# A decoder layer's layer norms read from PSUM on VectorE, and its output projection with two chunks per weight

## The chip, the cores and the metric

The kernel runs on one core of a Trainium2 chip. The metric is the device time of one execution in microseconds. In the text TensorE is PE in the profile, VectorE is DVE, ScalarE is ACT, GpSimd is POOL, and SyncE, which issues the DMAs, is SP.

## What is computed

One layer of a decoder trunk on 1056 tokens (1024 of a prompt, 32 of eight samples), width 1024, in float32:

```
x = LN1(alpha*x + 0.5*SwiGLU_1(x))         # FFN width 2816
m = mixer(x)                               # gMLP branch and gated DeltaNet branch, gated sum
x = LN2(alpha*x + m @ w_out)
y = LN3(alpha*x + 0.5*SwiGLU_2(x))

def layer_norm(x, g, b):
    mu = mean(x); var = mean((x - mu)**2)
    return (x - mu) * rsqrt(var + 1e-5) * g + b
```

## The kernel before

Activations lie with the features on the partitions: eight tiles of 128 features, each 1056 tokens wide. The tokens are cut into three chunks of `C` = 352. Chunk 2 (`LONE`) goes by itself, chunks 0 and 1 (`PAIR`) go together in the FFNs, where a scheme with fewer products combines both. Every product is made of three matmuls of a high and a low part (`mm3`: high by high, low by high, high by low), so every weight and every activation is split: `wh` is the rounded copy made by ScalarE, `wl` the rest, made by GpSimd or DVE. A unit is one weight of 128x1024 for one chunk, 24 matmuls.

The program is written out by one generator for all engines, in the order in which its own clock expects the work. Background generators (`ln_gen` is the one of a layer norm) are stepped between matmuls when that clock passes their due time, so the norm of one chunk is spread between the matmuls of the next. `tt()` gives an addition to GpSimd when its modelled end there, less a slack, is earlier, and to DVE else. At run time each engine goes through its own list in order.

There are nine layer norms: three norms by three chunks. Each works on the accumulator tile of its chunk (named `acc` in the first, `m` in the later norms), eight tiles of 128x352:

- `sum_step` adds the tiles, two at a time (704 wide), into `ss`, while the last products arrive; at the end the two halves of `ss` are added.
- A matmul of `ss` with a matrix of ones gives the column sums `mu` on every partition, in PSUM. ScalarE copies them, scaled by -1/1024, to `mus` in SBUF.
- Four additions of 704 columns subtract the mean (`tt()`, so DVE or GpSimd). ScalarE squares each into `lsq`; the four squares are added up, then the two halves.
- Three matmuls with a column of ones give the sums of squares per token, `vr` (128 tokens on partitions, three columns). DVE computes the inverse root on 128x3 tiles in SBUF (`vx`, `vy`, `vt`): twelve operations, three Newton steps.
- DVE writes three diagonals `dg` (the identity times a column of `vy`), and three matmuls with ones spread them to every partition: `rs`. ScalarE copies `rs` to `rss`.
- Eight scalings by `rss` and the gain: six on DVE, two on GpSimd (a product and then gain and bias). `emit1`, `emit2` and `emit3` then add the bias and split or store the result: `x1h`/`x1l` for the mixer, `x2h`/`x2l` for FFN 2, `y` to HBM.

The norms that matter below: LN1 of chunks 0 and 1 falls into the start of the mixer, where the projections of chunk 2 run and then the small beta and decay projection (`bd`, 16 matmuls) of chunk 0 needs `x1l`. LN2 belongs to the output projection, which goes through the chunks in the order 2, 0, 1 and for each through the eight weights `wo`, 24 units. LN1 and LN3 of chunk 2 fall into the start of the pair's work (the pair starts). LN3 of chunks 0 and 1 is the tail, in which TensorE has nothing else to do.

Of the kernel before, what the change touches and what calls it, by code (L numbers as in the profile page):

```python
# [12 lines left out]
F32 = mybir.dt.float32  # L13
# [8 lines left out]
P = 128  # L22
# [4 lines left out]
NC = 3  # L27
# [12 lines left out]
S0, S1 = 0.2, 0.4  # L40
NPL = 2, 2, 2
# [219 lines left out]
class Kern:  # L261
    def __init__(self, nc, tc, I, O, scratch=None):
# [8 lines left out]
        self.sct, self.scw, self.scn, self.vdone, self.zdone, self.odone, self.omm = {}, {}, {}, 0, 0, 0, 0  # L271
        self.n = 0
# [164 lines left out]
    def sum_step(self, f, c):  # L437

        if f % 2 == 0 or f == 1:
            return  # L440
# [1739 lines left out]
```

## Time and profile before

| | us |
|---|---|
| median of 3 runs | 2880.83 (2880.27 to 2881.67) |
| profiled execution | 2885.94 |
| its span | 2884.2 |
| TensorE busy | 2757.4 (96%) |
| DVE, ScalarE, GpSimd busy | 1746.9, 1110.6, 1449.5 |

The span is the time from the first to the last instruction that the profiler recorded; 1.7 us of the profiled execution lie outside it. Busy is the sum of an engine's instructions, and idle time counts only where the engine that sets the end (here TensorE nearly everywhere) waits for another.

### The profile page before, as it was taken

Reading aid. Unit: us, or ns where it says so; the run is one execution under the profiler, and the core shown is the slowest. Engines: PE = TensorE matmul, PEld = TensorE weight load, DVE = VectorE, ACT = ScalarE, POOL = GpSimd, SP = SyncE. Lnnn points to the kernel's source line nnn. Section 1 sums busy time; section 2 is a strip of 40 time slices with the busy share of each in tenths; the row PEclk is TensorE's granted clock in tenths of the full one; section 3 lists DMA queues with packets and bytes.
Section 4 is the critical chain, followed back from the end, with each engine's and each line's share of the span. In section 5 each row is a group of like instructions: output and inputs, shape, how many; then the busy total and the mean of one; then the engine's idle time right before and its main releaser. Section 6 shows DMA issues by size and latency. Waiting matters only on the chain. (4 is left out here: it accounts for less than half of the span.)

```text
span 2884.2 us, 44396 instructions
## 1 busy us (share of the span) xinstructions
PE 2757.4 (96%) x17467; PEld 2712.6 (94%) x17467; DVE 1746.9 (61%) x2602; ACT 1110.6 (39%) x2215; POOL 1449.5 (50%) x836
## 2 busy tenths in 40 slices
PE   8998999999899998998999999999989989999995
PEld 8998899999899998997999999999989989999995
DVE  4645765554867978997355445036885467554546
ACT  4433433333435655322542433224443334334332
POOL 5556665666526554344124133142466566656663
PEclk9999999999999999999999999999999999999997
DMA  6343122212237988433435287375334422322211
GB/s 228 129 155 97 59 94 74 88 59 74 77 88 161 183 188 155 129 112 133 118 109 165 87 293 268 125 255 188 125 110 139 139 88 65 96 65 88 75 58 40
DMA packets 236863, 358.98 MB, mean 124 GB/s; under 512 B 72144, under 2 KB 169040, under 8 KB 236272
## 3 DMA queue, kind: packets, MB, share of 16 engines
q1 hardware_dynamic: 236656, 356.16, 41.2%
q8 instruction: 137, 2.24, 0.3%
q14 instruction: 70, 0.57, 0.1%
HBM read 279.19 MB, written 76.91 MB: 123 GB/s over the span
## 5 line engine op out<-in xcount | busy, mean ns | idle before, releaser
L166 POOL TENSOR_TENSOR wl<-w,wh 128x1024 fp32r<-128x1024 f32 x220 | 563.8, 2573 | 779.4 <-ACT wh L166 589.4
L386 PE MATMUL ps<-x1h,wh 128*128 128x352 f32 x1536 | 514.7, 335 | 0.0
L388 PE MATMUL ps<-x1h,wl 128*128 128x352 f32 x1536 | 500.6, 326 | 2.2 <-POOL wl L166 2.2
L387 PE MATMUL ps<-x1l,wh 128*128 128x352 f32 x1536 | 499.8, 325 | 0.0
L388 PE MATMUL ps<-h,wl 128*128 128x352 f32 x1056 | 342.3, 324 | 4.6 <-POOL wl L166 4.6
L166 POOL TENSOR_TENSOR s<-w,s 128x512 fp32r<-128x512 f32 x168 | 234.7, 1410 | 218.8 <-ACT s L166 218.8
L386 PE MATMUL ps<-h,wh 128*128 128x352 f32 x1056 | 343.3, 325 | 0.3 <-ACT h L166 0.3
L166 ACT CAST wh<-w 128x1024 fp32r<-128x1024 f32 (+1 forms) x257 | 262.5, 1042 | 90.4 <-PE ps L387 49.8
L386 PEld LDWEIGHTS ps<-x1h,wh 128*128 128x128 f32 x1536 | 292.7, 191 | 4.8 <-issue 1.4
L388 PEld LDWEIGHTS ps<-x1h,wl 128*128 128x128 f32 x1536 | 292.1, 190 | 3.1 <-POOL wl L166 3.1
L387 PEld LDWEIGHTS ps<-x1l,wh 128*128 128x128 f32 x1536 | 292.5, 190 | 0.1
L387 PE MATMUL ps<-h,wh 128*128 128x352 f32 x704 | 228.2, 324 | 0.9 <-DVE h L166 0.9
L166 ACT CAST s<-w 128x512 fp32r<-128x512 f32 x220 | 130.8, 617 | 203.7 <-DVE w L166 101.5
L388 PEld LDWEIGHTS ps<-h,wl 128*128 128x128 f32 x1056 | 198.8, 188 | 5.9 <-POOL wl L166 5.9
L386 PEld LDWEIGHTS ps<-h,wh 128*128 128x128 f32 x1056 | 199.0, 188 | 1.4 <-ACT h L166 0.9
L386 PE MATMUL A<-T,s 128*128 128x352 f32 x528 | 174.5, 331 | 19.2 <-ACT T L166 6.6
L387 PE MATMUL A<-T,s 128*128 128x352 f32 x528 | 172.6, 327 | 1.0 <-DVE T L166 1.0
L388 PE MATMUL A<-T,s 128*128 128x352 f32 x528 | 172.5, 327 | 0.0
L166 DVE TENSOR_TENSOR p<-p,B 128x352 f32<-128x352 f32 x44 | 22.9, 520 | 222.5 <-PE B L388 222.5
L166 DVE TENSOR_TENSOR m<-m,ps 128x352 f32<-128x352 f32 x248 | 120.3, 514 | 54.3 <-PE ps L388 54.0
L387 PEld LDWEIGHTS ps<-h,wh 128*128 128x128 f32 x704 | 132.9, 189 | 1.4 <-DVE h L166 1.4
L166 DVE TENSOR_TENSOR acc<-acc,ps 128x352 f32<-128x352 f32 x224 | 108.0, 514 | 40.6 <-PE ps L388 40.5
(470 smaller groups left out, 7156.6 us busy)
## 6 DMA issues: line engine op xcount, KB each, us to landing
w<-in_wu SPq DMA_DIRECT2D x176, 512.0 KB
w<-in_wd SPq DMA_DIRECT2D x88, 512.0 KB
w<-in_wm SPq DMA_DIRECT2D x64, 512.0 KB
w<-in_wo SPq DMA_DIRECT2D x24, 512.0 KB
acc<-in_xt SPq DMA_DIRECT2D x12, 352.0 KB
scr_x<-acc SPq DMA_DIRECT2D x12, 352.0 KB
scr_z<-z SPq DMA_DIRECT2D x24, 176.0 KB
scr_ga<-tg SPq DMA_DIRECT2D x24, 176.0 KB
```

The lines of the kernel that those rows point to most:

```text
L166: return f(*a, **kw)
L386: nc.tensor.matmul(ps[:, :C], lh, xh, start=(start and i == 0), stop=False, skip_group_check=not start)
L387: nc.tensor.matmul(ps[:, :C], lh, xl, start=False, stop=False, skip_group_check=not start)
L388: nc.tensor.matmul(ps[:, :C], ll, xh, start=False, stop=(i == n - 1), skip_group_check=not start)
```

## The change

The layer norm is rewritten, and the output projection reordered:

- `sum_step` and all sums of squares are on DVE, none on GpSimd. In the very last norm (LN3 of chunk 1) the two halves of `ss` and of the squares are not added: `mu` and `vr` take each half in a matmul of its own.
- The subtraction reads `mu` straight from PSUM, on DVE, with the factor -1/1024 in the same operation. `mus` is gone.
- The inverse root keeps `x` and `t` in unused columns of the PSUM tile `vr`; only `y` is in SBUF. The count of operations stays at twelve, with the operands of a Newton step in another order.
- The diagonals are gone: `rs` comes from a matmul whose stationary operand is a column of `y` spread by its access pattern and whose moving operand is the identity.
- All eight scalings are on DVE and read `rs` from PSUM. `rss` is gone. GpSimd's share of the bias goes to ScalarE.
- The output projection does chunk 2 with the eight weights, and then chunks 0 and 1 together, each weight for both: 16 units loaded and split, not 24. The factor 0.5 moves from the split to the addition of the result (`m<-ps,m`).

Over the whole program: DVE gets 36 subtractions from PSUM where it had 21 and GpSimd 15, 27 sums of squares 704 wide (17 and 10), 72 scalings (54, GpSimd 18), no diagonals (27), and no scaled weight splits (24). ScalarE loses 9 `mus`, 9 `rss` and 24 scaled weight copies for 16 plain ones. GpSimd makes 234 of the weight splits, not 220. SyncE issues eight loads of 512 KB fewer. TensorE has the same 15,312 large matmuls.

```diff
@@ rsqrt
-            nc.vector.tensor_tensor(out=t, in0=y, in1=y, op=ALU.mult)
-            nc.vector.scalar_tensor_tensor(out=t, in0=t, scalar=-0.5, in1=x, op0=ALU.mult, op1=ALU.mult)
+            nc.vector.tensor_tensor(out=t, in0=x, in1=y, op=ALU.mult)
+            nc.vector.scalar_tensor_tensor(out=t, in0=t, scalar=-0.5, in1=y, op0=ALU.mult, op1=ALU.mult)
@@ sum_step
-        self.tt(self.ssum[c], self.acc4(0, c)[:, 0:2] if f == 3 else self.ssum[c], a, ALU.add, S0)
-        if f == 7:
-            self.tt(self.ssum[c][:, 0], self.ssum[c][:, 0], self.ssum[c][:, 1], ALU.add, 0.0)
+        v = self.nc.vector
+        v.tensor_tensor(out=self.ssum[c], in0=self.acc4(0, c)[:, 0:2] if f == 3 else self.ssum[c], in1=a, op=ALU.add)
+        if f == 7 and not self.ending(c):
+            v.tensor_tensor(out=self.ssum[c][:, 0], in0=self.ssum[c][:, 0], in1=self.ssum[c][:, 1], op=ALU.add)
@@ ln_gen
+        halves = 2 if which == 2 and c == ORD[-1] else 1
-        nc.tensor.matmul(mu[:, :C], self.ones, self.ssum[c][:, 0], start=True, stop=True)
+        for i in range(halves):
+            nc.tensor.matmul(mu[:, :C], self.ones, self.ssum[c][:, i], start=(i == 0), stop=(i == halves - 1))
-        mus = self.small("mus")
-        nc.scalar.activation(mus, mu[:, :C], AF.Copy, scale=-1.0 / 1024)
...
+        mub = mu[:, :C].unsqueeze(1).to_broadcast([P, 2, C])
+        for i in range(4):
+            a = self.acc4(i // 2, c)[:, i % 2 * 2:i % 2 * 2 + 2]
+            v.scalar_tensor_tensor(out=a, in0=mub, scalar=-1.0 / 1024, in1=a, op0=ALU.mult, op1=ALU.add)
...
-        x, y, t = self.tiny("vx", 3), self.tiny("vy", 3), self.tiny("vt", 3)
+        y = self.tiny("vy", 3)
+        x, t = vr[:, 8:11], vr[:, 16:19]
-        dg = [self.small("dg", P) for _ in range(3)]
-        for i in range(3):
-            v.tensor_scalar(out=dg[i], in0=self.ident, scalar1=y[:, i:i + 1], scalar2=None, op0=ALU.mult)
-        yield slack[2]
+        yield 1.2 + slack[2]
-            nc.tensor.matmul(rs[:, o:o + n], self.ones, dg[i][:, 128 - n:128], start=True, stop=True)
+            nc.tensor.matmul(rs[:, o:o + n], y[:, i:i + 1].to_broadcast([P, P]), self.ident[:, 128 - n:128], start=True, stop=True)
-        rss = self.small("rss")
-        nc.scalar.copy(rss, rs[:, :C])
...
+            v.scalar_tensor_tensor(out=a, in0=a, scalar=self.prm[:, o:o + 1], in1=rs[:, :C], op0=ALU.mult, op1=ALU.mult)
@@ mix_specs
-        for c in range(NC):
+        for i in range(2):
             for j in range(8):
-                out.append((I["wo"][j].rearrange("p k c -> p (k c)"), 1024, 0.5, ("o", c * 8 + j)))
+                out.append((I["wo"][j].rearrange("p k c -> p (k c)"), 1024, 1.0, ("o", i * 8 + j)))
@@ mixer, output projection
-        for i, c in enumerate(ORD):
+        for i, cs in enumerate(((LONE,), PAIR)):
...
+                for c in cs:
+                    def evac_o(ps, f=f, c=c):
+                        a = self.accv(f, c)
+                        v.scalar_tensor_tensor(out=a, in0=ps[:, 0:C], scalar=0.5, in1=a, op0=ALU.mult, op1=ALU.add)
+                        self.sum_step(f, c)
+                    self.unit_piece(ui, MM, c, evac_o)
```

Three places in DVE's list, before and after. The first is the tail, from the last additions of chunk 1 to the first inverse root; `m_277x` and `m_275x` are the accumulators, `ps` a finished product. Before:

```order
L166 TENSOR_TENSOR m_2780_17932<-m_2780_17932,ps_26819 128x352
L166 TENSOR_TENSOR m_2779_17931<-m_2779_17931,mus_26842 128x2x352
L166 TENSOR_TENSOR m_2780_17932<-m_2780_17932,mus_26842 128x2x352 x2
L166 TENSOR_TENSOR m_2780_17932<-m_2780_17932,ps_26832 128x352
L166 TENSOR_TENSOR ss_4105_26827<-ss_4105_26827,m_2780_17932 128x704
L166 TENSOR_TENSOR m_2780_17932<-m_2780_17932,ps_26847 128x352
L166 TENSOR_TENSOR m_2780_17932<-m_2780_17932,ps_26866 128x352
L166 TENSOR_TENSOR ss_4105_26827<-ss_4105_26827,m_2780_17932 128x704
L166 TENSOR_TENSOR ss_4105_26827<-ss_4105_26827 128x352
L166 TENSOR_TENSOR lsq_26851<-lsq_26851,lsq_26853 128x704
L166 TENSOR_TENSOR lsq_26851<-lsq_26851 128x352
L166 TENSOR_TENSOR m_2779_17931<-m_2779_17931,mus_26890 128x2x352
```

After:

```order
L164 TENSOR_TENSOR m_2759_17890<-m_2759_17890,ps_26729 128x352
L164 TENSOR_TENSOR ss_4034_26691<-ss_4034_26691,m_2759_17890 128x704
L164 TENSOR_TENSOR lsq_26706<-lsq_26706,lsq_26707 128x704
L164 TENSOR_TENSOR lsq_26706<-lsq_26706,lsq_26708 128x704
L164 TENSOR_TENSOR lsq_26706<-lsq_26706,lsq_26707 128x704
L164 TENSOR_TENSOR lsq_26706<-lsq_26706 128x352
L164 SCALAR_TENSOR_TENSOR m_2758_17889<-mu_26749,m_2758_17889 128x2x352 x2
L164 SCALAR_TENSOR_TENSOR m_2759_17890<-mu_26749,m_2759_17890 128x2x352 x2
L164 TENSOR_TENSOR lsq_26752<-lsq_26752,lsq_26753 128x704
L164 TENSOR_TENSOR lsq_26752<-lsq_26752,lsq_26754 128x704
L164 TENSOR_SCALAR vr_26763<-vr_26763 128x3 x2
L164 TENSOR_SCALAR vy_26769<-vr_26763 128x3
```

Before, three subtractions of chunk 0 stood ahead of chunk 1's last two sums, a fourth was on GpSimd, and the squares of chunk 0 were added up partly there. After, all four subtractions are in this list ahead of the rows shown, all sums of squares too, and the 352-wide sum of `ss` is gone.

The second place is the start of the mixer, behind the inverse root of LN1 of chunk 0. `x1l` is the low part of the normalised chunk 0, and `lsq_739x` and `lsq_734x` are sums of squares of chunk 1. Before:

```order
L166 TENSOR_TENSOR acc_1_83<-acc_1_83,mus_7355 128x2x352
L166 TENSOR_TENSOR acc_2_84<-acc_2_84,mus_7355 128x2x352
L166 TENSOR_TENSOR lsq_7391<-lsq_7391,lsq_7392 128x704
L166 SCALAR_TENSOR_TENSOR acc_1_83<-acc_1_83,prm,rss_7441 128x352 x4
L166 SCALAR_TENSOR_TENSOR acc_2_84<-acc_2_84,prm,rss_7441 128x352 x2
L166 TENSOR_TENSOR wl_1133_7463<-w_1112_7341,wh_1132_7462 128x1024
L166 TENSOR_TENSOR lsq_7393<-lsq_7393,lsq_7392 128x704
L166 SCALAR_TENSOR_TENSOR x1l_1137_7497<-acc_1_83,prm,x1h_1136_7481 128x352 x4
L166 SCALAR_TENSOR_TENSOR x1l_1137_7497<-acc_2_84,prm,x1h_1136_7481 128x352
L166 TENSOR_TENSOR lsq_7391<-lsq_7391,lsq_7393 128x704
L166 TENSOR_TENSOR lsq_7391<-lsq_7391 128x352
L166 SCALAR_TENSOR_TENSOR x1l_1137_7497<-acc_2_84,prm,x1h_1136_7481 128x352
```

After:

```order
L164 TENSOR_TENSOR lsq_7345<-lsq_7345,lsq_7346 128x704
L164 TENSOR_TENSOR lsq_7345<-lsq_7345,lsq_7347 128x704
L164 TENSOR_TENSOR lsq_7345<-lsq_7345,lsq_7346 128x704
L164 TENSOR_TENSOR lsq_7345<-lsq_7345 128x352
L164 SCALAR_TENSOR_TENSOR acc_1_83<-acc_1_83,prm,rs_7442 128x352 x4
L164 SCALAR_TENSOR_TENSOR acc_2_84<-acc_2_84,prm,rs_7442 128x352 x4
L164 SCALAR_TENSOR_TENSOR x1l_1122_7472<-acc_1_83,prm,x1h_1121_7466 128x352 x4
L164 TENSOR_SCALAR vr_7476<-vr_7476 128x3 x2
L164 TENSOR_SCALAR vy_7488<-vr_7476 128x3
```

Before, six scalings and six `x1l` stood here among chunk 1's sums, and chunk 1's inverse root came behind the last `x1l`. After, all sums of chunk 1's squares come first, then eight scalings, four `x1l`, and chunk 1's inverse root (from the last row on, twelve operations) ahead of the other four.

The third place is the start of FFN 2, with LN2 of chunks 0 and 1; `u` and `h` are the SiLU of chunk 2. Before, behind the inverse root of chunk 0:

```order
L166 TENSOR_SCALAR dg_19754<-cst,vy_19738 128x128
L166 SCALAR_TENSOR_TENSOR u_19792<-t_19791,ps_19692 128x352
L166 TENSOR_TENSOR u_19792<-u_19792,ps_19723 128x352
L166 SCALAR_TENSOR_TENSOR h_3006_19683<-u_19792,h_3006_19683 128x352
L166 TENSOR_TENSOR m_2779_17931<-m_2779_17931,mus_19775 128x2x352
L166 TENSOR_TENSOR m_2780_17932<-m_2780_17932,mus_19775 128x2x352 x2
L166 SCALAR_TENSOR_TENSOR m_2779_17931<-m_2779_17931,prm,rss_19818 128x352 x4
L166 SCALAR_TENSOR_TENSOR m_2780_17932<-m_2780_17932,prm,rss_19818 128x352 x2
L166 TENSOR_TENSOR lsq_19798<-lsq_19798,lsq_19799 128x704
L166 TENSOR_TENSOR wl_3043_19879<-w_3014_19721,wh_3042_19878 128x1024
```

After, from the `mu` of both chunks on:

```order
L164 TENSOR_TENSOR wl_2951_19564<-w_2936_19439,wh_2950_19563 128x1024
L164 SCALAR_TENSOR_TENSOR m_2758_17889<-mu_19596,m_2758_17889 128x2x352 x2
L164 SCALAR_TENSOR_TENSOR m_2759_17890<-mu_19596,m_2759_17890 128x2x352 x2
L164 SCALAR_TENSOR_TENSOR m_2758_17889<-mu_19625,m_2758_17889 128x2x352 x2
L164 SCALAR_TENSOR_TENSOR m_2759_17890<-mu_19625,m_2759_17890 128x2x352 x2
L164 TENSOR_TENSOR lsq_19608<-lsq_19608,lsq_19609 128x704
L164 SCALAR_TENSOR_TENSOR u_19664<-t_19663,ps_19571 128x352
L164 TENSOR_TENSOR u_19664<-u_19664,ps_19604 128x352
L164 SCALAR_TENSOR_TENSOR h_2947_19558<-u_19664,h_2947_19558 128x352
L164 TENSOR_TENSOR lsq_19608<-lsq_19608,lsq_19610 128x704
L164 TENSOR_TENSOR lsq_19608<-lsq_19608,lsq_19609 128x704
```

Before, the norm of chunk 0 had begun in the output projection, and the one of chunk 1 followed it. After, both begin in FFN 2, with the subtractions of both chunks in one row. At the two pair starts, in the same way, the eight scalings of chunk 2's norm now stand in the list between a SiLU's product with `p` and its product with `A`.

## Rows read from the trace of the kernel before

**Rows 1.** The page, busy time of each engine, share of the span, instructions.

```profile
PE 2757.4 (96%) x17467; PEld 2712.6 (94%) x17467; DVE 1746.9 (61%) x2602; ACT 1110.6 (39%) x2215; POOL 1449.5 (50%) x836
```

**Rows 2.** TensorE's waits in the whole run: us in total, times, longest.

```profile
PE rs L508 <- DVE dg L166: 24.6, 8, 8.2
```

**Rows 3.** Timeline of the tail: start us, us, engine, line, operation; idle time in brackets.

```profile
2842.56 4.01 DVE L166 TENSOR_TENSOR m<-m,mus 128x704 f32<-128x704 f32 x3 [1.05 <-ACT mus L166]
...
2845.58 0.32 PE L388 MATMUL ps<-h,wl 128*128 128x352 f32 x1
...
2845.80 1.47 ACT L166 ACTIVATE lsq<-m 128x704 f32<-128x704 f32 x2 [1.46 <-DVE m L166]
...
2852.33 1.54 PE L457 MATMUL mu<-ss,cst 128*128 128x352 f32 x2 [6.44 <-DVE ss L166]
...
2865.08 1.44 PE L496 MATMUL vr<-cst,lsq 128*128 128x1 f32 x6
...
2873.42 5.14 POOL L166 TENSOR_TENSOR m<-m,rss 128x352 f32<-128x352 f32 x1 [4.62 <-ACT rss L166]
...
2874.40 3.06 DVE L166 SCALAR_TENSOR_TENSOR m<-m,prm,rss 128x352 f32<-128x352 f32 x6
...
2875.08 2.06 ACT L166 ACTIVATE y<-m,prm 128x352 f32<-128x352 f32 x4 [1.09 <-DVE m L166]
...
2881.26 0.41 SPq L2093 DMA_DIRECT2D out_y<-m  x1
```

**Rows 4.** DVE operations by form: ns min/median/max, first and last start us.

```profile
L166 DVE TENSOR_TENSOR m<-m,ps x248: 504/514/524, 1985.8 to 2849.5; 128x352 f32<-128x352 f32 x124
...
L166 DVE SCALAR_TENSOR_TENSOR m<-m,prm,rss x36: 573/580/2724, 2040.9 to 2876.9; 128x352 f32<-128x352 f32 x36
...
L166 DVE TENSOR_TENSOR m<-m,mus x14: 877/886/2398, 2020.5 to 2857.5; 128x704 f32<-128x704 f32 x14
...
L166 DVE SCALAR_TENSOR_TENSOR vt<-vt,vx x30: 160/161/2267, 353.2 to 2869.8; 128x3 f32<-128x3 f32 x27, 128x9 f32<-128x9 f32 x3
...
L166 DVE TENSOR_SCALAR vx<-vr x9: 147/152/161, 349.9 to 2866.6; 128x3 f32<-128x3 f32 x9
```

**Rows 5.** Start of the mixer: TensorE's waits, two windows (busy, count, clock), DVE's timeline.

```profile
PE rs L508 <- DVE dg L166: 5.0, 1, 5.0
...
PE ps L413 <- DVE x1l L166: 4.0, 4, 2.0
...
778.80:785.60 6.80, 3.77 (x14) 3.77 (x15) 6.47 (x15) 2.60 (x5) 2.57 (x2) 0.50 0.00 0
...
792.50:806.10 13.60, 11.60 (x41) 9.15 (x41) 7.27 (x22) 0.55 (x1) 1.44 (x2) 0.50 0.01 1
...
770.57 0.46 DVE L166 TENSOR_TENSOR lsq<-lsq 128x352 f32<-128x352 f32 x1
...
772.14 2.34 DVE L166 TENSOR_SCALAR vt<-vx 128x3 int32<-128x3 int32 x1
...
796.59 0.58 DVE L166 SCALAR_TENSOR_TENSOR x1l<-acc,prm,x1h 128x352 fp32r<-128x352 f32 x1
```

**Rows 6.** Output projection and start of FFN 2: TensorE's waits, one window.

```profile
PE rs L508 <- DVE dg L166: 6.1, 3, 3.6
...
PE ps L388 <- DVE wl L166: 2.6, 3, 1.3
...
PE ps L388 <- POOL wl L166: 2.4, 3, 1.5
...
2123.70:2130.50 6.80, 4.36 (x16) 4.37 (x17) 5.80 (x17) 1.75 (x3) 0.67 (x1) 0.50 0.00 1
```

**Rows 7.** First pair start: TensorE's waits, the window behind them.

```profile
PE A L386 <- ACT p L166: 3.2, 2, 2.3
...
PE rs L508 <- DVE dg L166: 0.6, 1, 0.6
...
359.00:365.80 6.80, 5.91 (x20) 5.91 (x21) 5.91 (x8) 3.89 (x7) 5.32 (x5) 0.50 0.27 100
```

More of the change, by code (lines that the diff above doesn't have):

```diff
@@ L486, in ln_gen @@
-        self.cur = self.pet
-        self.tt(sq[2], sq[2], sq[1], ALU.add, S1)
-        yield (max(ends[2], self.cur),)
-        self.cur = self.pet
-        self.tt(sq[0], sq[0], sq[2], ALU.add, S1)
-        self.tt(sq[0][:, 0], sq[0][:, 0], sq[0][:, 1], ALU.add, 0.0)
+                v.tensor_tensor(out=sq[0], in0=sq[0], in1=sq[(0, 1, 2, 1)[i]], op=ALU.add)
+        if halves == 1:
+            v.tensor_tensor(out=sq[0][:, 0], in0=sq[0][:, 0], in1=sq[0][:, 1], op=ALU.add)
         yield (self.cur + slack[1],)
@@ L495, in ln_gen @@
         for i, o in enumerate((0, 128, C - 128)):
-            nc.tensor.matmul(vr[:, i:i + 1], sq[0][:, 0, o:o + 128], self.ones[:, 0:1], start=True, stop=True)
+            for k in range(halves):
+                nc.tensor.matmul(vr[:, i:i + 1], sq[0][:, k, o:o + 128], self.ones[:, 0:1], start=(k == 0), stop=(k == halves - 1))
         self.pe(1, 0.65)
         yield
-        x, y, t = self.tiny("vx", 3), self.tiny("vy", 3), self.tiny("vt", 3)
+        y = self.tiny("vy", 3)
+        x, t = vr[:, 8:11], vr[:, 16:19]
         v.tensor_scalar(out=x, in0=vr[:, 0:3], scalar1=1.0 / 1024, scalar2=1e-5, op0=ALU.mult, op1=ALU.add)
         self.rsqrt(y, x, t)
-        dg = [self.small("dg", P) for _ in range(3)]
-        for i in range(3):
-            v.tensor_scalar(out=dg[i], in0=self.ident, scalar1=y[:, i:i + 1], scalar2=None, op0=ALU.mult)
-        yield slack[2]
+        yield 1.2 + slack[2]
         rs = self.ps("rs")
         for i, (o, n) in enumerate(((0, 128), (128, 128), (256, 96))):
-            nc.tensor.matmul(rs[:, o:o + n], self.ones, dg[i][:, 128 - n:128], start=True, stop=True)
+            nc.tensor.matmul(rs[:, o:o + n], y[:, i:i + 1].to_broadcast([P, P]), self.ident[:, 128 - n:128], start=True, stop=True)
         self.pe(3, 0.218)
         yield
-        rss = self.small("rss")
-        nc.scalar.copy(rss, rs[:, :C])
-        yield
-        t, ends = self.cur, []
-        npl = NPL[which]
+        ends = []
         for f in range(8):
@@ L2046, in norm_x @@
             if s == 0:
-                if b is None:
-                    nc.scalar.copy(X.hi(f, c), z)
-                else:
-                    nc.scalar.activation(X.hi(f, c), z, AF.Identity, bias=b)
-            elif b is None:
-                nc.gpsimd.tensor_tensor(out=X.lo(f, c), in0=z, in1=X.hi(f, c).bitcast(F32), op=ALU.subtract)
+                nc.scalar.activation(X.hi(f, c), z, AF.Identity, bias=b)
             else:
@@ L2081, in emit2 @@
                 norm_x(X2, s, f, c, z, b)
-                if s and b is not None:
+                if s:
                     nc.scalar.activation(z, z, AF.Identity, bias=b)
             elif s == 0:
-                if b is not None:
-                    nc.scalar.activation(z, z, AF.Identity, bias=b)
+                nc.scalar.activation(z, z, AF.Identity, bias=b)
                 whole[0] += 1 / 16
@@ L2161, in build, with side2 @@
             return
-        half(n, X2, waiter(1), laster(2, emit3), lambda j: None, lambda n: [], lambda: None)
+        def side2():
+            self.ended = True
+        half(n, X2, waiter(1), laster(2, emit3), lambda j: None, lambda n: [], side2)
         self.flush()
```

66 lines of the change are left out of this document (19 added, 47 removed).

## The prediction

> **What bounds the kernel now.** I read the page's busy shares first: TensorE works 96% of the span, DVE 61%, ScalarE 39%, GpSimd 50% [rows 1]. The change leaves TensorE's large matmuls alone (15,312 before and after), so it can only win where TensorE stands still. The view of TensorE's waits shows which stops belong to the layer norms: 24.6 us in eight stops are for the diagonals that DVE writes ahead of `rs` [rows 2], and one of 6.44 for the sum ahead of the last `mu` [rows 3]. [...] Four places hold nearly all of it: the tail, the start of the mixer, the output projection with the start of the second FFN, and the two pair starts.
>
> **What the operations cost.** DVE's 128x352 addition of a PSUM tile takes 514 ns (504 to 524 in 248 cases, never longer), the scaling with two SBUF tensors 580 ns at the median but up to 2724, the 704-wide subtraction 886 up to 2398, and even the 128x3 operations go from 161 up to 2267 [rows 4]. The long ones coincide with GpSimd's work; the ones that read PSUM show none. Back to back an operation starts about 0.08 us less than its duration after the one before (six scalings of 0.58 in 3.06 us [rows 3]). My estimates for the new forms, from these rows:
> - subtraction reading `mu` from PSUM, 704 wide: 0.88 - 0.08 = 0.80 us, without the stretching;
> - scaling reading `rs` from PSUM: 0.51 - 0.08 = 0.43 us, nearest row the 514;
> - a 128x3 operation: 0.16 us, 0.2 from start to start (0.04 between them is my estimate), so 2.4 us for the chain of twelve.
>
> No row shows an operation that both reads and writes PSUM, which the shift and the first two steps of each iteration now do. The `vx` that reads PSUM took 152 ns (147 to 161), the ones in SBUF 161 [rows 4]; I take 0.16, nearest to both, and twice that as the upper bound; below, nothing but the 0.01 between the two rows is to be had.
>
> [...]
>
> **Tail: gain 7 (4 to 9).** Before, the last large matmul ends at 2845.90. The last chunk's sums stand behind three subtractions that take 4.01 us with what is between them, so `mu` starts at 2852.33 after its wait of 6.44. Later a GpSimd scaling stretches to 5.14 us and the last output is issued at 2881.26, 2.94 before the span ends [rows 3]. After, DVE's queue in the printed order:
> - four subtractions of the first chunk, from about 2842.1 (no ScalarE copy ahead; it was 2842.56): 2845.3;
> - three additions from PSUM (0.43) and two sums (0.82), the last bank ready at about 2846.4: 2848.3. `mu` now takes both halves, so the 352-wide sum is gone: it starts 3.7 us earlier than 2852.33;
> - three `lsq` sums and a short one, 3.0: 2851.3; four subtractions of the second chunk, 3.2: 2854.5;
> - its squares follow on ScalarE (two in 1.47 [rows 3]) and two sums on DVE: 2856.3; first chain 2.4: 2858.7; last sum: 2859.5;
> - six `vr` matmuls at half clock; before, three took 1.44 us (six hardware passes), so 2.9, DVE waiting: 2862.4; second chain: 2864.8;
> - sixteen scalings, 6.9: 2871.7. Fifteen of the sixteen bias additions go to ScalarE at 2.06/4 = 0.515 [rows 3], 7.7 from 2865.9: 2873.6, which is the later.
>
> So the last issue falls near 2874 instead of 2881.3. Bounds: 9 if the biases keep up, 4 if the 24 operations of the two chains take twice as long (3.8 more, less what the squares hide).
>
> **Start of the mixer: gain 5 (0 to 7).** TensorE waits 5.0 for the diagonals and 4.0 for `x1l`, and two stretches run at 0.50. The first chunk's chain is stretched by GpSimd (2.34 for one 128x3 operation) and its last `x1l` starts at 796.59 and ends at 797.2 [rows 5]. Before, the last `lsq` sum starts at 770.57 [rows 5]. After, one 704-wide sum more stands ahead of it (0.8) and four subtractions behind it (3.2), then the chain (2.4): 770.57 + 0.8 + 0.5 + 3.2 + 2.4 = 777.5. TensorE comes to this `rs` 18 large matmuls (2.8 us) later in its order, and the chain loses its stretched operations (2.2 us on the one shown, and more such), so the wait of 5.0 goes. But all of the second chunk's `lsq` sums (3.0), eight scalings (3.5) and its chain (2.4) now stand ahead of the last four `x1l` (0.58 - 0.08 = 0.5 each, 2.0 for four): 777.5 + 3.0 + 3.5 + 2.0 + 2.4 + 2.0 = 790.4, and 0 to 3 more beside GpSimd's splits. The wait moves from `rs` to `x1l`, and the half-clock stretch behind it stays. The beta and decay projection, which needs that `x1l`, ends 3.8 to 6.8 earlier. Upper bound 7; lower bound nothing, if GpSimd stretches the `lsq` sums and `x1l` as it did the chain.
>
> **Output projection and start of FFN 2: gain 9 (3 to 13).** TensorE waits 6.1 for diagonals, 2.6 and 2.4 for `wl` [rows 6], 11.1 together, and there is one stretch of 6.8 us at 0.50 in which TensorE was busy 4.36, worth half of that, 2.2. Sixteen units of `wo` are split instead of 24, and the 24 DVE splits go; that takes the `wl` waits inside the projection, while those in FFN 2, behind splits that stay, may stay too. The two remaining chunks now run their norms together in FFN 2: eight subtractions in one row (6.4), six `lsq` sums, two chains. From `mu` to `vr` of chunk 0 TensorE has 99 matmuls, 99 x 0.158 = 15.6 us (2757.4 us for 17,467 [rows 1]); DVE needs 6.4 + a split 1.2 (1024 wide, from the 0.88 for 704) + four sums 3.0 + three SiLU operations 1.6 = 12.2, and 0 to 5 beside GpSimd. I take four us of waits left in all: 11.1 + 2.2 less 4 is 9. Bounds: 13 with none left, 3 if all but the projection's waits come back.
>
> **Pair starts: gain 1 each (-3 to +3.5).** TensorE waits twice, 3.2 us in all, for ScalarE's `p` at the first start, and 6.8 us follow at 0.50 with 5.91 busy [rows 7]; the second start has the same waits without the slow stretch. The 0.6 for diagonals goes at each. But the eight scalings (3.5 us) now stand inside a SiLU's DVE chain, between its products with `p` and with `A`, so a later `A` is released as late as before. Either slow stretch may come or go, hence the bounds.
>
> **What costs nothing.** The 61 norm operations taken from GpSimd, the 18 ScalarE copies and 24 casts lie beside TensorE, which none of them stops except at the places above. The added eight bias activations too; without that cover each is 0.5 us of ScalarE. Eight `wo` loads fewer: what TensorE waits for in the projection is the splits, not the loads [rows 6]. The extra hold of a PSUM bank (`mu` for 3.2 us, `rs` for 3.5, where a copy freed it) is covered while TensorE has other banks of its eight; without cover it is a wait of that length at each norm, which is the rival below.
>
> **Sum.** 7 + 5 + 9 + 2 = 23. The profiled execution took 2885.94 us, 5.1 above the median of the runs, 2880.83; I take the 23 off both: 2862.9 profiled, **2858** timed.
>
> **Rivals.**
> - *The waits only move (0.20).* DVE now carries every norm alone, and its queue becomes what TensorE waits on: for it speak the moved `x1l` and the SiLU chain, against it the missing stretching. Mixer and FFN 2 give nothing back, the tail 7: 2874.
> - *PSUM in and out is dear (0.10).* If a 128x3 operation on PSUM takes 0.16 more, a chain is 1.9 longer: 3.8 at the tail, 1.9 to 3.8 at the mixer, 1 to 2 in FFN 2: gain 15, 2866. [...]
> - *It does nothing measurable (0.08).* The tail's chain waits on the second `vr` anyway and the moved waits eat the rest: within 2 to 5 of before, 2878.
> - *Slower (0.07).* Both norms at FFN 2's start hold DVE past the 15.6 us: from there on `vr` and `rs` of both chunks stop TensorE, four times. Priced at the one stop of this kind in the rows (5.0, and 1.9 for half of the 3.77 busy at 0.50 [rows 5]): 4 x 6.9 = 27.6 in place of 13.3, and the same lag costs 6 at the two pair starts and gives nothing at the mixer; with the tail's 7: about 13 more, 2894.
>
> **Chances and range.** My forecast holds 0.55. A difference under 0.2% (5.8 us) is about what a measurement of this kernel cannot tell from none. Faster: 0.55 + 0.10 and 0.13 of the first rival, 0.78; same: 0.07 of it, 0.08, 0.15; slower 0.07. The range goes from all upper bounds short of their coincidence (9 + 7 + 13 + 4 = 33, 2848) to the first rival's time, 2875, leaving out its far half and the last two.
>
> **What would show it.** Right: in the profile after, `mu` of the last chunk starts near 2848.6 and the last output issue near 2874; no wait of `rs` at the mixer's start and one for `x1l` of some 8 to 11 us instead; DVE operations on `mu`, `rs` and `vr` without the long cases; no `wl` wait in the projection. Wrong: 128x3 operations on `vr` well over 0.16; TensorE's `vr` and `rs` in FFN 2 waiting more than 6 us together; new waits for a PSUM bank behind the eight subtractions; another slow stretch at a pair start.

## The result

Over four runs each the changed kernel took 2849.86 us (2847.34 to 2856.87), the kernel before 2880.65 (2880.27 to 2881.67). The ratio is 0.9889 with a 95% interval of 0.9877 to 0.9901: 1.1% faster, some 31 us. Forecast were 23 us and 2858; the time lies inside the range, near its lower end.

The page after, busy times (compare [rows 1]):

```profile
PE 2754.6 (97%) x17475; PEld 2715.7 (95%) x17475; DVE 1688.0 (59%) x2600; ACT 1102.8 (39%) x2202; POOL 1382.8 (49%) x782
```

DVE, which took over all the norm's work from GpSimd, is busy for 59 us less than before. Of these, 31.8 us are the 24 scaled weight splits and 9.6 the 27 diagonals that are gone; and the new operations are not stretched: before, 54 scalings took 41.8 us, now 72 take 36.0. TensorE's waits in the whole run, those that concern the norms (us in total, times, longest; compare [rows 2]):

```profile
PE vr L487 <- DVE lsq L164: 10.0, 5, 6.6
...
PE A L385 <- ACT p L164: 7.6, 2, 4.3
...
PE mu L461 <- DVE ss L164: 2.7, 1, 2.7
...
PE rs L497 <- DVE vy L164: 1.1, 1, 1.1
```

The 24.6 us for `rs` are 1.1. What is left of `vr` (8.5 of the 10.0) and `mu` is in the tail, where a part of the wait has only changed its name: before, TensorE waited there 12.3 us for `rs` and 6.4 for `mu`, now 8.5 for `vr`, 2.7 for `mu` and 1.1 for `rs`. The durations of the new forms on DVE (ns min/median/max; compare [rows 4]):

```profile
L164 DVE SCALAR_TENSOR_TENSOR m<-mu,m x24: 877/880/892, 2006.4 to 2826.0; 128x704 f32<-128x704 f32 x24
...
L164 DVE SCALAR_TENSOR_TENSOR m<-m,prm,rs x48: 567/573/581, 2026.1 to 2844.2; 128x352 f32<-128x352 f32 x48
...
L164 DVE TENSOR_TENSOR vr<-vr,vy x27: 169/170/170, 344.1 to 2836.4; 128x3 f32<-128x3 f32 x27
```

Not one of them is stretched: maxima of 892, 581 and 170 where before stood 2398, 2724 and 2267. The tail (timeline; compare [rows 3]):

```profile
2813.88 3.28 DVE L164 SCALAR_TENSOR_TENSOR m<-mu,m 128x704 f32<-128x704 f32 x4 [0.55 <-PE mu L461]
...
2817.39 0.32 PE L387 MATMUL ps<-h,wl 128*128 128x352 f32 x1
...
2820.36 1.45 PE L461 MATMUL mu<-ss,cst 128*128 128x352 f32 x4 [2.65 <-DVE ss L164]
...
2831.79 2.72 PE L487 MATMUL vr<-cst,lsq 128*128 128x1 f32 x12 [6.64 <-DVE lsq L164]
...
2836.84 7.95 DVE L164 SCALAR_TENSOR_TENSOR m<-m,prm,rs 128x352 f32<-128x352 f32 x16
...
2838.07 7.90 SPq L2071 DMA_DIRECT2D out_y<-y  x16
...
2845.56 0.41 SPq L2071 DMA_DIRECT2D out_y<-y  x1
```

From the end of the last large matmul (2817.71) to the end of the span (2848.6) are 30.9 us, before 38.3 (2845.90 to 2884.2). TensorE's waits in the other three places: the start of the mixer (compare [rows 5]), the projection with the start of FFN 2 ([rows 6]), the first and the second pair start ([rows 7]):

```profile
PE ps L412 <- DVE x1l L164: 4.7, 2, 3.0
...
PE vr L487 <- DVE lsq L164: 1.1, 1, 1.1
...
PE A L385 <- ACT p L164: 3.3, 1, 3.3
...
PE A L385 <- ACT p L164: 4.3, 1, 4.3
```

The stretches at the lower clock behind them, in windows (busy and count of TensorE, weight loads, DVE, ScalarE, GpSimd, then the granted clock):

```profile
782.00:791.40 9.40, 6.94 (x24) 4.39 (x25) 6.04 (x21) 1.96 (x4) 0.00 (x0) 0.50 0.24 85
2095.40:2098.60 3.20, 3.20 (x13) 3.20 (x13) 2.95 (x7) 3.05 (x6) 1.97 (x1) 0.50 0.57 168
357.80:361.60 3.80, 3.80 (x15) 3.80 (x16) 0.02 (x1) 1.32 (x3) 2.37 (x1) 0.55 0.67 257
2416.90:2422.90 6.00, 5.42 (x18) 5.42 (x19) 0.00 (x0) 3.26 (x7) 2.37 (x1) 0.50 0.17 60
```

DVE's timeline at the start of the mixer:

```profile
771.48 4.12 DVE L164 TENSOR_TENSOR lsq<-lsq,lsq 128x704 f32<-128x704 f32 x3
775.63 2.60 DVE L164 TENSOR_TENSOR lsq<-lsq 128x352 f32<-128x352 f32 x1
778.16 4.01 DVE L164 SCALAR_TENSOR_TENSOR acc<-acc,prm,rs 128x352 f32<-128x352 f32 x8
...
786.36 2.06 DVE L164 SCALAR_TENSOR_TENSOR x1l<-acc,prm,x1h 128x352 fp32r<-128x352 f32 x4
```

At the mixer the wait for `rs` is gone and the one for `x1l` stays, as forecast; but the two slow stretches (3.77 and 11.60 us busy) have become one with 6.94 busy. Of what still reads SBUF twice, a sum of squares of 352 columns takes 2.60. In the projection no wait for `wl` is left. At the pair starts there is one wait for `p` each instead of two, but a longer one, and now both are followed by a slow stretch; before, only the first was. The new one, at the second start, is one of the signs of being wrong that the prediction named.

### The profile page after: what moved, and what is told of

The parts are those of the page before. It is cut to its first block, busy times and chain, and to the rows that moved or that the text cites. A ratio compares the mean times of both kernels' runs of the same rounds, so it can differ in the third digit from the quotient of the medians.

```text
span 2848.6 us, 44347 instructions
## 1 busy us (share of the span) xinstructions
PE 2754.6 (97%) x17475; PEld 2715.7 (95%) x17475; DVE 1688.0 (59%) x2600; ACT 1102.8 (39%) x2202; POOL 1382.8 (49%) x782
## 5 line engine op out<-in xcount | busy, mean ns | idle before, releaser
L164 POOL TENSOR_TENSOR wl<-w,wh 128x1024 fp32r<-128x1024 f32 x234 | 601.6, 2581 | 926.4 <-ACT wh L164 646.3
L164 ACT CAST wh<-w 128x1024 fp32r<-128x1024 f32 (+1 forms) x273 | 278.3, 1041 | 97.4 <-PE ps L386 58.9
L164 DVE TENSOR_TENSOR m<-m,ps 128x352 f32<-128x352 f32 x224 | 107.9, 514 | 44.0 <-PE ps L387 43.7
```

Source lines behind the costliest of these rows:

```text
L164: return f(*a, **kw)
```

## The experiments

All are compared with the kernel before on the chip that they ran on, in three groups of four on three chips. There the kernel before took 2891.5, 2891.6 and 2889.6 us (median), 9 to 11 more than in the first measurement, and scattered from 2883 to 2895; so ratios are compared, and 0.001 is 2.9 us. An interval is about 0.0015 to either side. The changed kernel was measured once more, in the second group, as the mark for the others.

> The changed kernel itself once more, to stand beside the three kernels below on one chip. All theories: 0.989 of the kernel before, as in the first measurement, within its interval of 0.1%; the profile has the waits of the first one.

| kernel | ratio | interval | median us |
|---|---|---|---|
| changed kernel, first measurement | 0.9889 | 0.9877 to 0.9901 | 2849.9 |
| changed kernel again | 0.9888 | 0.9872 to 0.9905 | 2857.5 |
| new norms, projection of before | 0.9881 | 0.9867 to 0.9895 | 2855.3 |
| paired projection, norms of before | 0.9984 | 0.9975 to 0.9994 | 2886.7 |
| all on DVE, reading SBUF | 0.9942 | 0.9929 to 0.9955 | 2872.5 |
| inverse root in SBUF | 0.9911 | 0.9896 to 0.9925 | 2863.9 |
| mu and rs copied to SBUF | 0.9902 | 0.9887 to 0.9917 | 2861.5 |
| sums on GpSimd or DVE | 0.9886 | 0.9870 to 0.9903 | 2857.0 |
| diagonals back | 0.9892 | 0.9876 to 0.9909 | 2857.2 |
| two scalings on GpSimd | 0.9874 | 0.9858 to 0.9890 | 2851.7 |
| pair starts: scalings spread | 0.9860 | 0.9845 to 0.9875 | 2847.7 |
| that, and the mixer's start | 0.9848 | 0.9833 to 0.9862 | 2843.6 |
| that, and the tail | 0.9842 | 0.9827 to 0.9856 | 2843.6 |

**Norms or projection.** One kernel has the new norms and the old projection, one the reverse (the two hunks of the diff on `wo` and the loop over `ORD` taken back, or taken alone).

> The new layer norms, with the output projection of before (24 units, chunks 2, 0, 1 one after another). Theory 1, norms that read PSUM keep their short durations beside GpSimd, and that is most of the gain: 20 to 27 us faster than before, with the waits for wl in the projection (2.3 us) back. Theory 2, it is enough that the norm's work has left GpSimd: the same here. Theory 3, the paired projection gives most: less than 12 us faster.

> The paired output projection alone, with the norms of before. Theories 1 and 2: 2 to 8 us faster than before, since the waits for diagonals at the mixer's start, in FFN 2 and at the tail stay (24.6 us in the run before). Theory 3: more than 15 us faster, and the stretch from the projection into FFN 2 gains some 14 us as in the changed kernel.

Measured: 0.9881 and 0.9984. The new norms alone give the whole gain, some 34 us and more than the 20 to 27 expected of them; the paired projection alone gives 0.16%, and on top of the norms nothing that can be measured. Theory 3 is out. With the old projection, its 24 units and the new norms, the stretch from the projection into FFN 2 has these waits:

```profile
PE vr L487 <- DVE lsq L164: 0.8, 1, 0.8
PE ps L387 <- POOL wl L164: 0.8, 1, 0.8
```

So of the 5.0 us for `wl` [rows 6] 4.2 go without one split being saved, and against what was expected they do not come back with the old projection. In the kernel with the paired projection alone, 3.7 us for `wl` on GpSimd stay in this stretch. That fits splits that were late because they stood behind the norm's work on DVE and GpSimd.

**Reading PSUM, or GpSimd out of the norms.** All norm work stays on DVE, but reads SBUF (`mub` is spread from `mus`, the scalings read `rss`):

```diff
-        mub = mu[:, :C].unsqueeze(1).to_broadcast([P, 2, C])
+        mus = self.small("mus")
+        nc.scalar.activation(mus, mu[:, :C], AF.Copy, scale=-1.0 / 1024)
+        yield
+        mub = mus.unsqueeze(1).to_broadcast([P, 2, C])
...
-            v.scalar_tensor_tensor(out=a, in0=mub, scalar=-1.0 / 1024, in1=a, op0=ALU.mult, op1=ALU.add)
+            v.tensor_tensor(out=a, in0=a, in1=mub, op=ALU.add)
...
-        x, t = vr[:, 8:11], vr[:, 16:19]
+        x, t = self.tiny("vx", 3), self.tiny("vt", 3)
...
+        rss = self.small("rss")
+        nc.scalar.copy(rss, rs[:, :C])
+        yield
...
-            v.scalar_tensor_tensor(out=a, in0=a, scalar=self.prm[:, o:o + 1], in1=rs[:, :C], op0=ALU.mult, op1=ALU.mult)
+            v.scalar_tensor_tensor(out=a, in0=a, scalar=self.prm[:, o:o + 1], in1=rss, op0=ALU.mult, op1=ALU.mult)
```

> The changed kernel with all norm work still on DVE, but reading SBUF: ScalarE copies mu and rs out of PSUM as before, and x and t of the inverse root are in SBUF tiles. Theory 1: subtractions, scalings and 128x3 operations stretch again where GpSimd works (maxima over 2 us), waits for vr, rs or x1l return at the mixer's start and in FFN 2, and it is 10 to 20 us slower than the changed kernel. Theory 2, that GpSimd no longer takes part is what counts: within 4 us of the changed kernel, the copies costing 1 to 2 us at the tail.

Measured: 0.9942, 15 us slower than the changed kernel (0.9888 on the next chip), inside theory 1's 10 to 20. Operations stretch again, and each long one lies beside a GpSimd operation. An example, DVE's and GpSimd's timeline at the mixer's start:

```profile
780.75 2.39 DVE L164 TENSOR_TENSOR vt<-vx,vy 128x3 f32<-128x3 f32 x1
780.74 2.39 POOL L164 TENSOR_TENSOR wl<-w,wh 128x1024 fp32r<-128x1024 f32 x1 [0.25 <-DVE vy L164]
```

Counted over this kernel's trace, 8 of 36 subtractions, 5 of 72 scalings and 11 of 99 operations of the inverse root that read SBUF alone took more than 1.25 times their median. Every one of these 24 overlapped a GpSimd operation and ended a fixed time after that one's end: 0.75 us the subtractions, 0.38 the scalings, 0.01 to 0.03 the 128x3 operations. In the changed kernel 66 of the 216 operations that read PSUM in their place overlapped a GpSimd operation too, and none is long. The two halves apart:

> The changed kernel with x and t of the inverse root in SBUF tiles instead of columns of the PSUM tile, nothing else. Theory A, of the 15 us that reading SBUF cost the changed kernel (0.9942 against 0.9889 of before) most belongs to the 128x3 operations, which stand in chains of twelve and stretched to over 2 us each beside GpSimd: 8 to 15 us slower than the changed kernel. Theory B, most belongs to subtractions and scalings: 0 to 5 us slower. [...]

> The changed kernel with mu and rs copied to SBUF by ScalarE, subtractions and scalings reading the copies, and the 128x3 operations in PSUM as in the change. Theory A: 1 to 6 us slower than the changed kernel, of which about 1.5 at the tail for the copies. Theory B: 8 to 15 us slower, with subtractions and scalings up to 3 us long and waits for vr or x1l at the mixer's start.

Measured: 0.9911, some 6.5 us slower, and 0.9902, some 4. On this chip the changed kernel took 2856.8 to 2858.1, these two 2863.3 to 2864.9 and 2859.4 to 2863.6, so both are clear of it. Neither theory holds whole: the 4 are inside A's 1 to 6, but the 6.5 lie between A's 8 to 15 and B's 0 to 5, so both halves share the loss. That the whole costs more than the sum of the halves, 15 against 10.5, is not clear of the intervals. DVE's operations by form (ns min/median/max), in the kernel with the inverse root in SBUF:

```profile
L164 DVE SCALAR_TENSOR_TENSOR vy<-vt,vy x30: 161/161/2399, 345.6 to 2849.8; 128x3 f32<-128x3 f32 x27, 128x9 f32<-128x9 f32 x3
```

And in the one with the copies:

```profile
L164 DVE TENSOR_TENSOR m<-m,mus x24: 877/884/3117, 2016.3 to 2836.0; 128x704 f32<-128x704 f32 x24
...
L164 DVE SCALAR_TENSOR_TENSOR m<-m,prm,rss x48: 571/579/2758, 2038.8 to 2854.3; 128x352 f32<-128x352 f32 x48
```

The medians are those of the PSUM forms (884 to 880, 579 to 573, 161 to 170); only the long cases return, up to 3.1 us. The second kernel's 4 us are not the price of the stretching alone: ScalarE's copies add to the tail (1.5 us, by place below), and they also moved the scalings behind the SiLU at the pair starts, where its waits for `p` are shorter, so a gain found below is in it, as it is in the kernel that reads SBUF throughout. Only the first kernel has no copies; its 6.5 us are the memory's alone. At the tail it gains nothing: 31.1 us there, the changed kernel's 31.2.

**The other parts of the norms.** The sums through `tt()` again (those of `ss` with a slack of 0.2), the diagonals again, and two of eight scalings on GpSimd, each in the changed kernel by itself.

```diff
-                v.tensor_tensor(out=sq[0], in0=sq[0], in1=sq[(0, 1, 2, 1)[i]], op=ALU.add)
+                self.tt(sq[0], sq[0], sq[(0, 1, 2, 1)[i]], ALU.add, 0.4)
```

> The changed kernel with the 704-wide sums of columns and of squares given to GpSimd or DVE by the generator's modelled end, as before; all else reads PSUM on DVE. Theory 1: 2 to 8 us slower than the changed kernel, from sums of 1.7 us on GpSimd in the chains and a few stretched DVE sums. Theory 2: 8 to 15 us slower, since GpSimd is back in every norm. Neither: no difference, if the sums are off the path.

```diff
-        yield 1.2 + slack[2]
+        dg = [self.small("dg", P) for _ in range(3)]
+        for i in range(3):
+            v.tensor_scalar(out=dg[i], in0=self.ident, scalar1=y[:, i:i + 1], scalar2=None, op0=ALU.mult)
+        yield slack[2]
...
-            nc.tensor.matmul(rs[:, o:o + n], y[:, i:i + 1].to_broadcast([P, P]), self.ident[:, 128 - n:128], start=True, stop=True)
+            nc.tensor.matmul(rs[:, o:o + n], self.ones, dg[i][:, 128 - n:128], start=True, stop=True)
```

> The changed kernel with the three diagonals per norm back on DVE (and rs from them by ones), all else as changed. If the spreading without diagonals is a real part of the gain: 3 to 8 us slower than the changed kernel, about 1.4 of it at the tail (two times 0.68), the rest where a diagonal, whose operands lie in SBUF, stretches beside GpSimd. Rival: the diagonals were only the last link of a late chain: within 2.5 us.

```diff
+        rss = self.small("rss")
+        nc.scalar.copy(rss, rs[:, :C])
+        yield
...
-            v.scalar_tensor_tensor(out=a, in0=a, scalar=self.prm[:, o:o + 1], in1=rs[:, :C], op0=ALU.mult, op1=ALU.mult)
+            if f < 6:
+                v.scalar_tensor_tensor(out=a, in0=a, scalar=self.prm[:, o:o + 1], in1=rss, op0=ALU.mult, op1=ALU.mult)
+            else:
+                nc.gpsimd.tensor_tensor(out=a, in0=a, in1=rss, op=ALU.mult)
+                nc.gpsimd.tensor_scalar(out=a, in0=a, scalar1=self.prm[:, o:o + 1], scalar2=None, op0=ALU.mult)
```

> The changed kernel with two of a norm's eight scalings back on GpSimd, product and gain, from a copy rss in SBUF that the other six on DVE read too (the bias stays on ScalarE). If taking GpSimd out of the norms matters by itself: 6 to 15 us slower than the changed kernel, of which some 4 at the tail, where a GpSimd product beside DVE's scalings took 5.14 us before. Rival: it costs only what reading rs from SBUF costs, some 2 to 4 us.

Measured: 0.9886, 0.9892 and 0.9874. Sums and diagonals make no difference in the whole that can be told: both of theory 1's and 2's numbers for the sums fail, and the rival on the diagonals holds by its number, but by place (below) losses and gains cancel in both. The third is not slower at all, some 4 us faster if anything. Its tail does cost the 4 that were expected (34.9 us from the last large matmul's end, not 30.9), but at the pair starts its profile has no wait for `p`: the copy to `rss` moves the scalings behind the SiLU in DVE's order. What GpSimd in the scalings costs elsewhere is not shown, since this kernel's scalings on DVE read SBUF as well.

**The row of eight.** That led to the pair starts. In the changed kernel DVE's timeline at the first:

```profile
350.20 1.18 DVE L164 SCALAR_TENSOR_TENSOR t<-t,p 128x352 f32<-128x352 f32 x1
...
351.30 4.01 DVE L164 SCALAR_TENSOR_TENSOR acc<-acc,prm,rs 128x352 f32<-128x352 f32 x8
355.23 0.50 DVE L164 TENSOR_TENSOR t<-t,A 128x352 f32<-128x352 f32 x1
```

ScalarE's, behind it:

```profile
355.83 0.50 ACT L164 ACTIVATE h<-t 128x352 fp32r<-128x352 f32 x1 [5.03 <-DVE t L164]
356.76 0.50 ACT L164 ACTIVATE h<-t 128x352 fp32r<-128x352 f32 x1 [0.44 <-DVE t L164]
357.17 0.43 ACT L164 COPY p<-A 128x352 f32<-128x352 f32 x1
```

And TensorE's:

```profile
357.65 0.47 PE L385 MATMUL A<-T,s 128*128 128x352 f32 x1 [3.32 <-ACT p L164]
```

The eight scalings hold DVE for 4 us between two operations of a SiLU. ScalarE's two `h` wait for that SiLU, the copy of `p` stands behind them in ScalarE's list, and TensorE's next matmul into `A`, at 357.65, comes when that copy has ended, at 357.60. The edit issues the scalings of chunk 2's first and third norm in four pairs, with a due time between them:

```diff
+        spread = c == LONE and which != 1
...
         for n in range(0, 8, 2):
+            if spread:
+                if n:
+                    yield 1.0
+                    self.cur = self.pet
+                scale((n, n + 1))
             yield (ends[n + 1],)
```

> The changed kernel with the eight scalings of chunk 2's norm at the two pair starts issued in four pairs between the SiLU's operations, nothing else moved. If the row of eight is what holds ScalarE's copy p there: both waits for p under 1.5 us, the slow stretches behind them gone, 5 to 9 us faster than the changed kernel (0.9888 of before on this chip). Rival: the copy waits for something else too, and it is within 2 us.

Measured: 0.9860, some 8 us faster. The same place in DVE's timeline of that kernel:

```profile
351.68 1.06 DVE L164 SCALAR_TENSOR_TENSOR acc<-acc,prm,rs 128x352 f32<-128x352 f32 x2
352.67 0.51 DVE L164 TENSOR_TENSOR t<-t,A 128x352 f32<-128x352 f32 x1
```

And what is left of TensorE's wait there, 0.4 for 3.3, and at the second start, 1.3 for 4.3, both under the 1.5 expected:

```profile
PE A L385 <- ACT p L164: 0.4, 1, 0.4
...
PE A L385 <- ACT p L164: 1.3, 1, 1.3
```

The clock behind these waits was read in the kernel that has the mixer's start and the tail moved as well, with the same 0.4 and 1.3 us of waits: 1.00 in every window of 4 us from 352 to 372 and from 2400 to 2440.

Then chunk 0's `rs` at the mixer's start is made due earlier (`yield 1.2` in place of 2.7), which puts its scalings and all its `x1l` ahead of chunk 1's inverse root; and in one kernel the tail is reordered too (chunk 0's `rs` due at 0.3, halves of the last sums added up on DVE again).

> The same, and at the mixer's start chunk 0's rs is due 1.5 us earlier, so that its scalings and x1l come ahead of chunk 1's last sums and inverse root; the tail as in the changed kernel. The kernel with the tail moved as well was 0.9842 of before; its tail took 31.7 us from the last large matmul to the end, the changed kernel's 31.2. So this one should be the same or up to 1 us faster: 0.983 to 0.985. Rival: the tail's moves did gain and the mixer's did not: 0.986 or more.

> The changed kernel with four moves in the order of work: at the two pair starts the eight scalings go in four pairs between the SiLU's operations; at the mixer's start chunk 0's scalings and x1l go ahead of chunk 1's last sums and its inverse root; at the tail chunk 0's rs and scalings go ahead of chunk 1's inverse root, and mu and vr take summed halves again. If the eight scalings in one row are what holds the next A at the pair starts, the waits for p (3.3 and 4.3 us) fall under 1.5 each and the slow stretches behind them shorten: 6 to 10 us. The mixer's wait for x1l falls from 4.7 to under 2: 3 to 6. The tail: 1 to 3. Together 8 to 18 us faster than the changed kernel. Rival: those waits have other causes, and moved work costs elsewhere: within 4 us of it.

Measured: 0.9848 and 0.9842. With the mixer's move the wait for `x1l` is 2.3 us (under 2 was expected). In the kernel with the tail moved too it is 2.1, and the granted clock there is 0.96 and 0.61 in the two windows of 4 us from 772 to 780 and 1.00 from 780 to 800. The intervals of the three kernels overlap, so the move's own share (some 3 us) is not shown beyond the profile; there the mixer's start gains 6.4 us, and the rest of the program is 4.4 longer. The tail's moves gave nothing: from the last large matmul's start at 2810.11 to the end of the span at 2841.8 are 31.7 us, in the changed kernel 31.2. While DVE scaled chunk 0, the second `vr` lay ready, and `rs` of chunk 1 then came with nothing beside it. Against the changed kernel the best version is some 13 us faster, 1.6% faster than before.

**By place.** Every trace holds 15,312 large matmuls, so a place can be timed in every kernel from the start of one to the start of another, counted from the first. The first pair start goes here from number 1860 to 2200, the mixer's start from 4360 to 4730, projection and FFN 2 from 10,000 to 12,100, the second pair start from 12,680 to 13,100, the tail from the last one to the end of the span; "rest" is all else (us, the one profiled execution of each kernel).

| kernel | first pair start | mixer's start | projection, FFN 2 | second pair start | tail | rest |
|---|---|---|---|---|---|---|
| before | 64.5 | 90.4 | 363.5 | 76.5 | 38.7 | 2250.7 |
| paired projection, norms of before | 63.3 | 87.6 | 360.3 | 77.1 | 38.7 | 2251.9 |
| changed kernel | 62.3 | 81.4 | 347.8 | 76.9 | 31.2 | 2249.0 |
| changed kernel again | 62.3 | 81.5 | 347.8 | 77.2 | 31.2 | 2255.7 |
| new norms, projection of before | 62.3 | 81.7 | 346.2 | 77.0 | 31.7 | 2256.2 |
| all on DVE, reading SBUF | 64.3 | 88.0 | 351.1 | 76.1 | 32.7 | 2258.5 |
| inverse root in SBUF | 65.9 | 82.0 | 349.8 | 81.2 | 31.1 | 2251.6 |
| mu and rs copied to SBUF | 62.8 | 85.7 | 349.3 | 74.5 | 32.7 | 2254.5 |
| sums on GpSimd or DVE | 64.7 | 82.4 | 344.7 | 78.1 | 30.6 | 2257.4 |
| diagonals back | 60.6 | 82.7 | 349.8 | 74.3 | 32.6 | 2256.3 |
| two scalings on GpSimd | 57.4 | 82.3 | 349.6 | 70.3 | 35.2 | 2251.5 |
| pair starts: scalings spread | 57.8 | 81.7 | 347.8 | 71.5 | 31.2 | 2253.9 |
| that, and the mixer's start | 57.8 | 75.3 | 347.8 | 71.7 | 31.2 | 2258.3 |
| that, and the tail | 57.8 | 76.2 | 347.8 | 71.7 | 31.7 | 2256.6 |

Both executions of the changed kernel agree within 0.4 us at each place, while the rest differs by 6.7. The kernel before is less steady: the one with the paired projection is the same program up to the projection, yet took 1.2 less at the first pair start and 2.8 less at the mixer's start. Read by place, the question of the theories has two answers. At the mixer's start all on DVE but reading SBUF (88.0) gives nothing over the norms of before (87.6 to 90.4): the gain there is the reading of PSUM, with the copies that it saves. In projection and FFN 2 and at the tail the same kernel keeps 12.4 of 15.7 and 6.0 of 7.5 us: most of the gain there does not need PSUM. And a total that stays the same can hide two effects. The diagonals cost 1.3, 2.0 and 1.4 us at the mixer's start, in FFN 2 and at the tail (1.4 was expected at the tail), and the same kernel gains 1.7 and 2.6 at the pair starts.

## Why the prediction was right, and where it was off

- **That only TensorE's waits could give time**: right. The mechanism was right too: operations that read PSUM keep their duration beside GpSimd (66 of 216 ran beside one, and none took more than 892 ns as a subtraction, 581 as a scaling and 170 in the inverse root). Shown by the kernel that reads SBUF, which gives back 15 of the 31 us, with the same medians and with long cases that each end with a GpSimd operation; but only about half of the gain hangs on it.
- **Durations**: 0.88 for the subtraction (880 measured) and 0.16 for a 128x3 operation (169 to 170) hold. The scaling does not: 573 ns, 0.50 from start to start, not 0.51 and 0.43. Its nearest row was the one with the same gain from `prm`, 573 at its least [rows 4], not the addition. At the tail sixteen took 7.95 us where 6.9 was worked out; the end was not later for it, since the forecast had ScalarE's biases end last anyway.
- **Tail, 7**: 7.4 measured. `mu` came 2.65 us after TensorE got there where 2.7 was worked out (2848.6 less 2845.9), and the last output was issued at 2845.56, 27.9 us after the last large matmul's end, where 28.1 was worked out (2874 less 2845.9).
- **Mixer's start, 5**: 9.0 by place. Waits and half of what ran at 0.50 made 9.0 + 7.7 = 16.7 before and 4.7 + 3.5 = 8.2 after (in the changed kernel a matmul took 0.29 us at 0.50, 24 in 6.94 busy, and 0.15 at 1.00, 40 in 6.00 from 797 to 803). The wait for `x1l` is 4.7, not 8 to 11, but the beta and decay projection ended 5.8 us earlier, inside the forecast's 3.8 to 6.8. Its last matmul, before and after (3.8 us of the difference had been gained ahead of this place):

```profile
798.38 0.49 PE L413 MATMUL ps<-x1l,wbd 128*16 128x352 f32 x1
...
788.73 0.49 PE L412 MATMUL ps<-x1l,wbd 128*16 128x352 f32 x1
```

  The step that failed is "the half-clock stretch behind it stays": with 4.7 us of waits, in two parts, it ended after 6.94 busy us in place of 15.4. Not all of that need be the change. In the kernel with the paired projection, up to here the same program as before, TensorE waited 5.0 and 3.8 us and the second stretch lasted 6.8 us where it had lasted 13.6; so 2.8 of the 9.0 may be the execution.
- **Projection and FFN 2, 9**: 15.7 by place, over the bound of 13. By the rows named it is about 10 (13.3 before; 1.1 of waits, 0.4 of smaller ones and half of 3.2 after, 3.1), with the smaller waits of before, 2.7, about 13; where the last 3 come from is not shown. The four us of waits that I left in were 1.5. But what the step said of the cause was wrong: it gave the `wl` waits to the paired units. The new norms alone take 4.2 of the 5.0 away, and the paired units alone leave 3.7. So the forecast of a gain here was right in part for a cause that was not the one.
- **Pair starts, +2**: 1.8 by place, 2.2 at the first start and -0.4 at the second. That it fits is luck. The slow stretch behind the first start is missing in the kernel with the paired projection, behind the same waits, and the second start has one that it had not: waits of 5.8 before, 4.3 and 2.7 of clock after. The text saw the scalings inside the SiLU and priced them at nothing new; without them both places would have gained, 4.5 and 5.4 us more, as the spread order shows.
- **Sum**: 2.2 + 9.0 + 15.7 - 0.4 + 7.5 = 34.0 of the 35.6 by which the profiled spans differ. The timed gain is 31: the profiled execution of the kernel before was 5.1 above its median, and 4.0 of the 34 are the first pair start and the mixer's start, where the same program has also been that much faster. The forecast's 23 was short mainly in FFN 2.
- **Rivals**: "the waits only move" came true in part, at the pair starts (for `p` 3.2 to 3.3 and 3.3 to 4.3) and at the tail, from `rs` to `vr`. PSUM in and out is not dear: 169 to 170 ns with input and output in PSUM against 161 in SBUF, and the tail with the inverse root in SBUF is 31.1 us for 31.2. The one that ends slower needed DVE more than 15.6 us late in FFN 2; TensorE waited 1.1 there.

What the runs leave open: 17 us lie between the kernel before and the one that has everything on DVE but reads SBUF (0.9942). By place they are in projection and FFN 2 (12.4) and at the tail (6.0). Of these the missing diagonals are worth 2.0 and 1.4, by the kernel that has them back, and the paired projection 3.2 in FFN 2 when it is alone and nothing on top of the norms. What remains was not tried apart; in it are 15 subtractions taken off GpSimd, which took 1.7 to 2.7 us each there. The sums, put back alone, cost nothing at these two places. The rest of the program differs by 6.7 us between two profiled executions of the changed kernel, so a difference of 4 us in the whole says little of one edit.

## What to carry to other kernels

If an engine's operations show a short median and a maximum many times that (here 161 and 2399 ns), ask with what they collide before asking how long they take: moving one operand to PSUM took no work away and made about half of the gain, 15 of 31 us. When a background job's eight operations are issued in one row (here 4.01 us of DVE between two operations of a SiLU), look at what foreground chain they cut, two engines further on; issued in pairs they left 0.4 and 1.3 us of the 3.3 and 4.3. And several edits that take away the same wait cannot be told apart by adding each alone: take each away from the whole as well, and time the places apart, since an edit that moves the order can gain at one what it loses at another.

## What the runs showed of the hardware that was not expected

- DVE operations with one operand in PSUM or with both input and output there were never stretched in the changed kernel: 36 subtractions 877 to 892 ns, 72 scalings 564 to 581, 108 operations of the inverse root at 155 to 170. The same operations on SBUF tiles went up to 3120 and 2781 in the kernel with everything on DVE but reading SBUF, and to 2399 in the one with the inverse root in SBUF. The sums of squares, which read SBUF twice, still reached 2887 ns in the changed kernel: of the 27 that are 704 wide, 8 took more than 1.25 times their median of 891, and each of the 8 ended 0.75 us after a GpSimd operation that it overlapped. A shift of 128x3 with one input in SBUF stretched too, to 2.34 us [rows 5]; in the kernel before, 4 of its 9 were long, each ending 0.02 to 0.03 us after a GpSimd operation.
- The slow stretch behind a stop was not in proportion to it, and not the same in two executions: 4.3 us of waiting for `p` in one piece left TensorE at 0.50 for 6.0 us; before, 3.3 us in two pieces at the same place left none, and 4.0 us for `x1l` in four pieces left 13.6 [rows 5]. In the kernel with the paired projection, the same program up to there, 3.8 us in four pieces left 6.8. Behind the first pair start, with the same 3.2 us in two pieces, it has the clock at 1.00 where the kernel before had 6.8 us at 0.50 [rows 7]. Its windows:

```profile
359.00:365.80 6.80, 6.80 (x44) 6.80 (x44) 6.80 (x8) 2.90 (x5) 6.59 (x5) 1.00 0.46 166
...
790.50:797.30 6.80, 4.96 (x16) 2.87 (x17) 3.88 (x6) 0.55 (x1) 1.17 (x1) 0.50 0.01 2
797.30:804.10 6.80, 6.80 (x47) 6.80 (x47) 2.63 (x15) 0.80 (x2) 0.00 (x0) 1.00 0.00 0
```
